# Modulation vectors of a hybrid encoder trunk, made in pairs with their columns in four blocks over the partitions

## The chip, the cores and the metric

The kernel runs on one core of a Trainium2 chip. A core has five engines with queues of their own: PE (TensorE, matrix products), DVE (VectorE), ACT (ScalarE), POOL (GpSimd) and SP (SyncE, which here issues the transfers). The metric is the device time of one execution in microseconds (us); a lower one is better.

## What is computed

Two layers over x of 1024 tokens by 1024 features. Layer 0 mixes tokens with forgetting attention (16 heads), layer 1 with gated linear attention (GLA, 4 heads); each mixer is followed by a SwiGLU with 2816 hidden features. Every sub-layer is normed and modulated by vectors that come from the conditioning vector `c`:

```python
c_act = jax.nn.silu(c)                                   # (1, 1024)
for i in range(DEPTH):                                   # 2 layers
    mod = c_act @ ada_w[i] + ada_b[i]                    # ada_w[i]: (1024, 6 * 1024)
    sh1, sc1, g1, sh2, sc2, g2 = jnp.split(mod, N_MOD, axis=-1)
    h = modulate(rms_norm(x, norm1_g[i]), sh1, sc1)      # h * (1 + sc1) + sh1
    y = mixer(h)
    x = x + g1[:, None, :] * y
    h = modulate(rms_norm(x, norm2_g[i]), sh2, sc2)
    x = x + g2[:, None, :] * swiglu(h, ffn_w_in[i], ffn_w_out[i])
return rms_norm(x, final_g)
```

The change is about `c_act @ ada_w[i]`: a vector of 1024 times a matrix of 1024 by 6144, for each layer. It is 25 MB of weights a layer, used once each, in float32.

## The kernel before

The time is mostly matrix products. Projections and the SwiGLU are done as three products of a high and a low half of each operand (`mm3`, L235 to L239), with the halves made by ACT and DVE (`split`, L159 and L160) or by ACT and POOL (`load_w`, L202 and L205). The SwiGLU (`ffn`) works with blocks whose sums and differences POOL forms from raw weights (L683 to L695); products are read out by ACT (L1410) and DVE (L1285). Weights come through `feed`, which makes them some loads ahead (`feed.depth`, 5 in the SwiGLU).

The modulation vectors are the weighted sum of the rows of `ada_w`. Vectors 0 and 1 of layer 0 are needed at once and are made by `ada0_mod`, which the change leaves alone. The others are made beside the main work by `ada_steps` (L336), one vector `j` at a time. A step `k` loads 128 rows of the matrix, one row for each partition, and multiplies each partition by its value of silu(c) (`cact[:, k:k+1]`), adding to `acc`. After the eight steps of a group, `acc` holds in each partition a partial sum, and PE adds over the partitions: `acc`'s 128 columns are the weights of a product with a column of ones (L377), which puts 128 results over the partitions, as the modulation needs them.

- Layer 0, vectors 2 to 5, in attention: a step is 128 x 1024 (512 KB, one transfer), in the ring `wr` that the weights use too; DVE multiplies and adds in four pieces of 256 columns (L367, L369). The queue `ada0` advances after each projection.
- Layer 1, vectors 0 and 1 in the SwiGLU of layer 0, vectors 2 to 5 in GLA: a group is 512 columns, a step is 128 x 512 (256 KB, one transfer, L345) into one of three buffers (SwiGLU) or two (GLA). ACT multiplies (L358 into `acc` for the first step, L360 in place for the others) and POOL adds to `acc` (L361). The load for the next step is issued ahead. The queue `ada1` is advanced by what each product is worth; a step counts `ADA_A` + `ADA_B`, 9 in the SwiGLU and 3.5 in GLA.

`acc` is one buffer in each stage. The result of L377 goes through DVE with the bias added (L379) to `modc`, and for vectors 1 and 4 `make_a` forms (1 + scale) times the norm's weight. All transfers are issued by SP, in order; an issue waits until its buffer is free. The program's order is written by hand, but the order on each engine is set at compile time by a scheduler that places work where it expects an engine to be free, so steps can run ahead of the place that the pace gives them.

At the start SP loads the first tokens of x, then rows of `c`, the biases and the norm weights (L290 to L298), which PE turns (L312, L313) so that `cact` can be made by ACT (L316).

Of the kernel before, what the change touches and what calls it, by code (L numbers as in the profile page):

```python
# [9 lines left out]
F32 = mybir.dt.float32  # L10
# [43 lines left out]
def trunk(ctx, tc, x, c, ada_w, ada_b, norm1_g, norm2_g, ffn_w_in, ffn_w_out,  # L54
          fox_w_in, fox_b_f, fox_w_out, gla_w_in, gla_w_a2, gla_b_a, gla_g_o,
          gla_w_out, final_g, out, dbg=None, stop=None):
    nc = tc.nc
    dbg = dbg or {}
    cst = ctx.enter_context(tc.tile_pool(name="cst", bufs=1))
# [49 lines left out]
    def psl(t, n=1):  # L109
        return slice(t * P, (t + n) * P)  # L110
# [40 lines left out]
    ones = cst.tile([P, 1], F32, name="ones")  # L151
    nc.vector.memset(ones, 1.0)
    mhalf = cst.tile([P, 8], F32, name="mhalf")
    nc.vector.memset(mhalf, -0.5)
    maskb = cst.tile([P, P], BF16, name="maskb")
    tri = cst.tile([P, P], I32, name="tri")

# [4 lines left out]
    wr = Ring(big, names[0:3])  # L162
# [96 lines left out]
    acc_r = Ring(big, acc_sl)  # L259
# [14 lines left out]
    def load_x(t):  # L274
        nc.sync.dma_start(xt[t], x[0, psl(t), :])
# [4 lines left out]
    def load_ada0(d):  # L280
        for kh in range(2):
# [2 lines left out]
                nc.sync.dma_start(t[:, :, j, :], adaw[0, :, 4 * kh:4 * kh + 4, j, d, :])  # L284
            araw[(d, kh)] = t

    load_x(0)
    rows2 = mrows[1][0:32]
    nc.vector.memset(rows2, 0.0)
# [40 lines left out]
    def make_a(l, i, ks=slice(0, 8)):  # L330
        j = 1 if i == 0 else 4
        g0 = 96 + i * 16 + l * 8
        nc.vector.scalar_tensor_tensor(amul[:, l, i, ks], modc[:, l, j, ks], 1.0,
                                       vec[:, g0:g0 + 8][:, ks], op0=ALU.add, op1=ALU.mult)

    def ada_steps(l, j, acc_of, raw_of, w):  # L336

        steps = deque((c0, k) for c0 in range(0, D, w) for k in range(8))
        got = deque()

        def load():
            if steps:
                c0, k = steps.popleft()
                raw = raw_of([P, w], F32, f"ada{l}{j}{c0}{k}")
                nc.sync.dma_start(raw, ada_w[l, psl(k), j * D + c0:j * D + c0 + w])  # L345
                got.append(raw)

        for c0 in range(0, D, w):
            acc = acc_of([P, w], F32, f"acc{l}{j}{c0}")
            for k in range(8):  # L350
                if w == D or c0 == k == 0:
                    load()
                raw = got.popleft()
                if w < D:
                    load()
                    yield ADA_A
                    if k == 0:
                        nc.scalar.mul(acc, raw, cact[:, 0:1])  # L358
                    else:
                        nc.scalar.mul(raw, raw, cact[:, k:k + 1])  # L360
                        nc.gpsimd.tensor_add(acc, acc, raw)  # L361
                    yield ADA_B
                    continue
                for q in range(0, w, 256):
                    cs = slice(q, q + 256)
                    if k == 0:
                        nc.vector.tensor_scalar(acc[:, cs], raw[:, cs], cact[:, 0:1], None, op0=ALU.mult)  # L367
                    else:
                        nc.vector.scalar_tensor_tensor(acc[:, cs], raw[:, cs], cact[:, k:k + 1], acc[:, cs],  # L369
                                                       op0=ALU.mult, op1=ALU.add)  # L370
                yield 1.0
            if w < D:
                yield ADA_B
            n, b = w // P, c0 // P
            mp = pj([P, n], F32, f"mp{l}{j}{c0}")
            for k in range(n):
                nc.tensor.matmul(mp[:, k:k + 1], acc[:, psl(k)], ones, start=True, stop=True)  # L377
            o = l * 48 + j * 8 + b
            nc.vector.tensor_add(modc[:, l, j, b:b + n], mp, vec[:, o:o + n])  # L379
            for i, jj in ((0, 1), (1, 4)):  # L380
                if j == jj:
                    make_a(l, i, slice(b, b + n))
        yield 1.0

    class Pace:
# [20 lines left out]

    ada0, ada1 = Pace(), Pace()

    def ada1_queue(js, acc, raws_, w):
        r = Cycle(raws_)  # L410
        for j in js:
            ada1.q.append(ada_steps(1, j, lambda *_: acc, r, w))

    mk = mrows[2]
    nc.vector.memset(mk, 0.0)
# [162 lines left out]
    sr, tr, orr, pj = ps_rings(2, 3, 1, 2)  # L578
# [229 lines left out]
    acc = first_acc(0)  # L808
# [37 lines left out]
    acc = first_acc(1)  # L846
# [1042 lines left out]
```

## Time and profile before

| | |
|---|---|
| median of 3 runs | 2449.29 us (2447.56 to 2454.5) |
| profiled execution, first to last instruction | 2446.2 us |
| transfers issued by SP for the vectors outside `ada0_mod` | 32 of 512 KB, 96 of 256 KB |
| products with ones (L377), records | 160, two for each product |
| POOL adds for the vectors (L361) | 84 |

The page gives the span of the profiled execution as its only time. Its parts are busy times of the engines, the chain of work that ended last, groups of instructions by line, and the transfers. A row of instructions reads: line, engine, operation, what it writes <- what it reads, count, then nanoseconds (least/median/most) or microseconds, and what it waited for. `issue` is time in which nothing visible was waited for.

### The profile page before, as it was taken

What the parts mean: (1) busy time and instruction counts of PE and PEld (TensorE: products, weight loads), DVE (VectorE), ACT (ScalarE), POOL (GpSimd) and SP (SyncE); (2) the same over time, 40 slices, a digit from 0 to 9 for tenths busy, and PEclk for the clock granted to TensorE, in tenths of its full rate; (3) what the DMA queues carried; (4) which work ended last, traced back from release to release, by engine and by line L of the source; (5) the groups of instructions that cost most, each with busy time, mean ns of one, the idle gap of its engine ahead of it and who ended that gap; (6) DMA issues with size and microseconds to landing.
All of it is one profiled execution on the core that took longest, in us unless ns stands there. A gap on an engine that the chain in (4) does not pass through costs nothing.

```text
span 2446.2 us, 35525 instructions
## 1 busy us (share of the span) xinstructions
PE 2385.6 (98%) x12458; PEld 2030.6 (83%) x12458; DVE 1701.0 (70%) x2849; ACT 1193.2 (49%) x2281; POOL 1151.3 (47%) x1006
## 2 busy tenths in 40 slices
PE   6999999999999999999999999999999999999998
PEld 5888888888887878888888888888888888888878
DVE  7577777676686777665788455446487677665787
ACT  4665565675454443335324765564354333345325
POOL 4233333333347786653363544443336656653262
PEclk9999999999999999999999999999999999999999
DMA  8223333223425544347665333335325434347664
GB/s 269 79 87 121 103 96 113 70 95 113 137 98 195 184 164 162 124 162 263 227 214 174 94 100 102 100 104 173 100 80 191 147 134 155 130 168 257 233 206 148
DMA packets 318203, 359.19 MB, mean 147 GB/s; under 512 B 18044, under 2 KB 246552, under 8 KB 318024
## 3 DMA queue, kind: packets, MB, share of 16 engines
q1 hardware_dynamic: 318024, 356.92, 43.7%
q8 instruction: 98, 1.61, 0.3%
q14 instruction: 81, 0.66, 0.1%
HBM read 268.19 MB, written 88.67 MB: 146 GB/s over the span
## 4 chain that ended last, share of the span: by engine, by line
PE 81%; DVE 7%; ACT 3%; DMA 3%; POOL 2%; issue 2%; SPq 1%; DVEq 0%; POOLq 0%; ACTq 0%
PE p_b L237 15%; PE p_b L239 14%; PE p_b L238 14%; PE o_b L947 2%; PE t_b L933 2%; PE qk_b L237 2%; PE qk_b L238 2%; PE qk_b L239 2%; DMA ad_s<-in_ada_w_dram 2%; PE s_b L902 1%; PE s_b L903 1%; POOL ad_s L361 1%; DVE o_s L160 1%; PE vps_b L237 1%; PE vps_b L239 1%
## 5 line engine op out<-in xcount | busy, mean ns | idle before, releaser
L160 DVE TENSOR_TENSOR o_s<-xv_s,o_s 128x512 fp32r<-128x512 f32 (+1 forms) x376 | 326.4, 872 | 86.8 <-ACT o_s L159 86.0
L159 ACT CAST o_s<-xv_s 128x512 fp32r<-128x512 f32 (+1 forms) x376 | 217.4, 587 | 308.2 <-PE p_b L239 258.5
L237 PE MATMUL p_b<-B,o_s 128*128 128x512 f32 x608 | 237.2, 393 | 7.3 <-DVE x L1285 4.9
L238 PE MATMUL p_b<-B,o_s 128*128 128x512 f32 x608 | 238.5, 392 | 0.0
L239 PE MATMUL p_b<-B,o_s 128*128 128x512 f32 x608 | 238.0, 392 | 0.0
L913 POOL TENSOR_SCALAR lp_s<-lp_s,st 128x128 f32<-128x128 f32 (+7 forms) x128 | 95.9, 754 | 294.9 <-DVE st L912 266.2
L683 POOL TENSOR_TENSOR ex_s<-xv_s,xv_s 128x512 f32<-128x512 f32 (+1 forms) x64 | 90.2, 1409 | 250.6 <-DMA xv_s<-in_ffn_w_in_dram 88.9
L237 PE MATMUL p_b<-T,o_s 128*128 128x512 f32 x480 | 187.6, 391 | 0.0
L238 PE MATMUL p_b<-T,o_s 128*128 128x512 f32 x480 | 186.9, 389 | 0.0
L239 PE MATMUL p_b<-T,o_s 128*128 128x512 f32 x480 | 182.1, 390 | 0.0
L237 PEld LDWEIGHTS p_b<-B,o_s 128*128 128x128 f32 x608 | 115.0, 189 | 32.4 <-DVE x L1285 4.2
L239 PEld LDWEIGHTS p_b<-B,o_s 128*128 128x128 f32 x608 | 115.1, 189 | 24.0
L238 PEld LDWEIGHTS p_b<-B,o_s 128*128 128x128 f32 x608 | 115.1, 189 | 23.6
L911 ACT ACTIVATE lp_s<-lp_s,st 128x128 f32<-128x128 f32 (+7 forms) x128 | 99.3, 776 | 56.3 <-DVE st L907 55.7
L1285 DVE TENSOR_TENSOR ex_s<-ex_s,p_b 128x512 f32<-128x512 f32 x140 | 94.0, 681 | 34.2 <-PE p_b L239 34.0
L159 ACT CAST pt_s<-t_b 128x512 fp32r<-128x512 f32 (+1 forms) x160 | 80.1, 547 | 71.4 <-PE t_b L933 70.2
L685 POOL TENSOR_TENSOR xv_s<-ex_s,xv_s 128x512 f32<-128x512 f32 (+1 forms) x64 | 83.5, 1305 | 63.0 <-DVE o_s L160 61.1
L160 DVE TENSOR_TENSOR pt_s<-t_b,pt_s 128x512 fp32r<-128x512 f32 (+1 forms) x160 | 96.5, 630 | 17.9 <-ACT pt_s L159 17.3
L239 PEld LDWEIGHTS p_b<-T,o_s 128*128 128x128 f32 x480 | 90.3, 188 | 19.0
L237 PEld LDWEIGHTS p_b<-T,o_s 128*128 128x128 f32 x480 | 90.2, 188 | 18.5
L238 PEld LDWEIGHTS p_b<-T,o_s 128*128 128x128 f32 x480 | 90.2, 188 | 18.4
L907 DVE CUSTOM_DVE_ANT_0 lp_s<-s_b,cum_s 128x512 f32<-128x512 f32 (+3 forms) x128 | 72.6, 569 | 40.6 <-PE t_b L933 23.0
(1939 smaller groups left out, 7543.3 us busy)
## 6 DMA issues: line engine op xcount, KB each, us to landing
xv_s<-in_ffn_w_in_dram SPq DMA_DIRECT2D x176, 256.0 KB, 3.0
hid_B<-x SPq DMA_DIRECT2D x70, 512.0 KB, 2.6
ad_s<-in_ada_w_dram SPq DMA_DIRECT2D x96, 256.0 KB, 2.9
hid_T<-x SPq DMA_DIRECT2D x36, 512.0 KB, 2.7
xv_s<-in_ffn_w_out_dram SPq DMA_DIRECT2D x96, 192.0 KB, 3.9
ada_s<-in_ada_w_dram SPq DMA_DIRECT2D x32, 512.0 KB, 3.8
xv_s<-in_ffn_w_out_dram SPq DMA_DIRECT2D x40, 256.0 KB, 2.8
T2o<-hid_T SPq DMA_DIRECT2D x18, 512.0 KB, 8.0
```

Source lines behind the costliest of these rows:

```text
L159: nc.scalar.copy(hi, src)
L160: nc.vector.tensor_sub(lo, src, hi.bitcast(F32))
L237: nc.tensor.matmul(ps, ah, bh, start=start, stop=False)
L238: nc.tensor.matmul(ps, ah, bl, start=False, stop=False)
L239: nc.tensor.matmul(ps, al, bh, start=False, stop=stop)
L683: nc.gpsimd.tensor_add(s1, a21, a22)
L685: nc.gpsimd.tensor_sub(a11, s1, a11)
L907: nc.vector.tensor_tensor_reduce(lp[:, k0:k1], ps, cm[:, k0:k1], 1.0, mcur, ALU.add, ALU.min, mnew)
L911: nc.scalar.activation(lp, lp, AF.Exp, bias=mcur, scale=-1.0, accum_out=st[:, qi, 2:3])
L913: nc.gpsimd.tensor_scalar(lp, lp, st[:, qi, 3:4], 1.0, op0=ALU.mult, op1=ALU.mult)
L933: nc.tensor.transpose(tp[:, i, :], lps[qi][:, psl(2 * b + jj)], ident)
L1285: nc.vector.tensor_add(d, d if src is None else dest(G, src), ps)
```

## The change

`ada_steps` becomes `ada_pair`: it makes two vectors, `j` and `j + 1`, together. Their 2048 columns are cut in four blocks `q` of 512. Partition 32 q + r holds block q, and it takes the 32 rows 32 r to 32 r + 31 of the matrix one after the other; a step `s` takes row 32 r + s in each. So a step is again 128 x 512 for layer 1 (and 128 x 1024, two rows, for layer 0), but a group is 32 rows long, a pair is one group, and a step's load is four transfers of 32 partitions each. The multiplier of a partition is silu(c[32 r + s]), held in a new tile `cblk` of 128 x 32, which four small loads of `c` on ACT's queue at the start and one more Silu fill. At the end PE adds over the 32 partitions of each block: the moving operand is `quart`, 128 x 4, with a one where the partition belongs to the block, so a product of 128 of `acc`'s columns gives four result columns. Four products finish a pair, where each vector took eight.

```diff
+    quart = cst.tile([P, 4], F32, name="quart")
+    nc.vector.memset(quart, 0.0)
+    for q in range(4):
+        nc.vector.memset(quart[32 * q:32 * q + 32, q:q + 1], 1.0)
...
+    craw = mrows[4][:, 0:32]
+    cblk = cst.tile([P, 32], F32, name="cblk")
+    for q in range(4):
+        nc.scalar.dma_start(craw[32 * q:32 * q + 32], c[0].rearrange("(r s) -> r s", s=32))
     load_x(0)
...
     nc.scalar.activation(cact, vps[:, P:P + 8], AF.Silu)
+    nc.scalar.activation(cblk, craw, AF.Silu)
...
-    def ada_steps(l, j, acc_of, raw_of, w):
+    def ada_pair(l, j, acc_of, raw_of, n):
+        steps = deque(range(0, 32, n))
         got = deque()
+        rows_ = ada_w[l, :, j * D:(j + 2) * D].rearrange("(r s) (q m) -> q r s m", s=32, q=4)
         def load():
             if steps:
+                s = steps.popleft()
+                raw = raw_of([P, n * HALF], F32, f"ada{l}{j}{s}")
+                for q in range(4):
+                    nc.sync.dma_start(raw[32 * q:32 * q + 32].rearrange("r (s m) -> r s m", s=n),
+                                      rows_[q, :, s:s + n])
+                got.append((s, raw))
+        acc = acc_of([P, HALF], F32, f"acc{l}{j}")
+        for i in range(0, 32, n):
+            if n > 1 or i == 0:
+                load()
+            s0, raw = got.popleft()
+            if n == 1:
+                load()
+                yield ADA_A
+                if i == 0:
+                    nc.scalar.mul(acc, raw, cblk[:, 0:1])
+                else:
+                    nc.scalar.mul(raw, raw, cblk[:, i:i + 1])
+                    nc.gpsimd.tensor_add(acc, acc, raw)
+                yield ADA_B
+                continue
+            for s in range(s0, s0 + n):
+                for c0 in range(0, HALF, 256):
...
+                        nc.vector.scalar_tensor_tensor(acc[:, cs], raw[:, rs_], cblk[:, s:s + 1], acc[:, cs],
                                                        op0=ALU.mult, op1=ALU.add)
+            yield 1.0
+        if n == 1:
+            yield ADA_B
+        mp = pj([P, 16], F32, f"mp{l}{j}")
+        for b in range(4):
+            nc.tensor.matmul(mp[:, b:16:4], acc[:, psl(b)], quart, start=True, stop=True)
+        o = l * 48 + j * 8
+        nc.vector.tensor_add(modc[:, l, j:j + 2, :].rearrange("p j k -> p (j k)"), mp, vec[:, o:o + 16])
+        if j in (0, 4):
+            make_a(l, j // 4)
...
-    for j in (2, 3, 4, 5):
-        ada0.q.append(ada_steps(0, j, acc_r, wr, D))
+    for j in (2, 4):
+        ada0.q.append(ada_pair(0, j, acc_r, wr, 2))
...
-        ada1_queue((0, 1), v[0], v[1:4], HALF)
+        ada1_queue((0,), v[0], v[1:4])
...
-    ada1_queue((2, 3, 4, 5), ada_v[0], ada_v[1:3], HALF)
+    ada1_queue((2, 4), ada_v[0], ada_v[1:3])
```

More of the change, by code (lines that the diff above doesn't have):

```diff
@@ L334, in make_a @@
                                        vec[:, g0:g0 + 8][:, ks], op0=ALU.add, op1=ALU.mult)
-    def ada_steps(l, j, acc_of, raw_of, w):
-        steps = deque((c0, k) for c0 in range(0, D, w) for k in range(8))
+    def ada_pair(l, j, acc_of, raw_of, n):
+        steps = deque(range(0, 32, n))
         got = deque()
+        rows_ = ada_w[l, :, j * D:(j + 2) * D].rearrange("(r s) (q m) -> q r s m", s=32, q=4)
         def load():
             if steps:
[L343 to L358, printed above, removed]
-                    else:
[L360 to L369, printed above, removed]
-                                                       op0=ALU.mult, op1=ALU.add)
[L371 to L382, printed above, removed]
@@ new lines, in load @@
+                s = steps.popleft()
[21 more added lines that the diff above has]
+                for c0 in range(0, HALF, 256):
+                    cs, rs_ = slice(c0, c0 + 256), slice((s - s0) * HALF + c0, (s - s0) * HALF + c0 + 256)
+                    if s == 0:
+                        nc.vector.tensor_scalar(acc[:, cs], raw[:, rs_], cblk[:, 0:1], None, op0=ALU.mult)
+                    else:
+                        nc.vector.scalar_tensor_tensor(acc[:, cs], raw[:, rs_], cblk[:, s:s + 1], acc[:, cs],
+                                                       op0=ALU.mult, op1=ALU.add)
+            yield 1.0
@@ L407, in trunk, with ada1_queue @@
     ada0, ada1 = Pace(), Pace()
-    def ada1_queue(js, acc, raws_, w):
+    def ada1_queue(js, acc, raws_):
         r = Cycle(raws_)
         for j in js:
-            ada1.q.append(ada_steps(1, j, lambda *_: acc, r, w))
+            ada1.q.append(ada_pair(1, j, lambda *_: acc, r, 1))
     mk = mrows[2]
```

## The prediction

> **What bounds the kernel now.** I read the page first: busy shares, then the chain that ended last.
>
> ```profile
> span 2446.2 us, 35525 instructions
> PE 2385.6 (98%) x12458; PEld 2030.6 (83%) x12458; DVE 1701.0 (70%) x2849; ACT 1193.2 (49%) x2281; POOL 1151.3 (47%) x1006
> ...
> PE 81%; DVE 7%; ACT 3%; DMA 3%; POOL 2%; issue 2%; SPq 1%; DVEq 0%; POOLq 0%; ACTq 0%
> ```
>
> PE is idle for 60 us of 2446 and holds 81% of the chain, so work taken from PE shortens the time unless a wait replaces it. The change touches the start and three stages, so I cut the span there (stretch, its length, busy time of each engine, then granted clock, DMA share and rate):
>
> ```profile
> 120.00:580.00 460.00, 452.65 (x2966) 397.93 (x2965) 344.95 (x908) 284.67 (x612) 163.28 (x228) 1.00 0.32 100
> 735.00:870.00 135.00, 128.71 (x562) 105.81 (x563) 94.34 (x112) 60.83 (x104) 103.49 (x70) 0.97 0.55 184
> 870.00:1060.00 190.00, 190.00 (x847) 157.57 (x846) 140.09 (x170) 76.91 (x131) 131.96 (x87) 1.00 0.45 153
> 1345.00:1660.00 315.00, 304.44 (x1863) 270.85 (x1863) 161.64 (x260) 194.40 (x398) 150.77 (x142) 0.99 0.33 101
> ```
>
> These are attention (layer 0 vectors), the SwiGLU of layer 0 (vectors 0 and 1 of layer 1; two stretches) and GLA (vectors 2 to 5). PE idles 7.4, 6.3, 0 and 10.6 us in them. PE is the bound in each; what idles lies in stretches in which vectors are being made (in the third the last of them are done by 915).
>
> **PE's products.** The products with the ones column are L377:
>
> ```profile
> L377 PE MATMUL mp_b<-ones,ad_s x96: 163/250/251, 755.2 to 1683.3; 128*128 128x1 f32 x96
> L377 PE MATMUL mp_b<-ones,acc_s x64: 164/250/251, 180.2 to 480.1; 128*128 128x1 f32 x64
> ...
> 1385.47 0.39 PE L239 MATMUL gk_b<-h1h,w_l_s 128*128 128x512 f32 x1
> 1385.70 0.95 PE L377 MATMUL mp_b<-ones,ad_s 128*128 128x1 f32 x8
> 1386.51 0.48 PE L237 MATMUL gk_b<-h1h,w_h_s 128*128 128x512 f32 x1
> ```
>
> 160 records are 80 products (two records each). The timeline shows what four of them cost: from 1385.70 to the next product's start at 1386.51 is 0.81 us. So 20 sets of four take 16.2 us now. After the change each of five pairs has four products, of four columns instead of one: 5 x 0.81 = 4.1 us. **PE gains 12.1 us**, spread over stages where it is the bound. I keep the price per product: the 128 weight columns are the same, and three more moving columns are little. Bounds of the saving: 10 us if a record with four columns cost 0.15 instead of 0.1 us, 13 us if part of the 0.81 is a hidden gap.
>
> **The transfers.** Each load becomes four, one for each 32 partitions: 128 issues on SP become 512, with the bytes unchanged.
>
> ```profile
> L345 SPq DMA_DIRECT2D ad_s<-in_ada_w_dram x96: 327/328/544, 708.6 to 1653.8; - x96
> ...
> 1.64 0.28 SPq L291 DMA_DIRECT2D mrows_s<-in_gla_g_o_dram  x1
> 1.96 0.29 SPq L292 DMA_DIRECT2D mrows_s<-in_gla_b_a_dram  x1
> 2.30 0.29 SPq L293 DMA_DIRECT2D mrows_s<-in_final_g_dram  x1
> ...
> ad_s<-in_ada_w_dram SPq DMA_DIRECT2D x96, 256.0 KB, 2.9
> ada_s<-in_ada_w_dram SPq DMA_DIRECT2D x32, 512.0 KB, 3.8
> ```
>
> An issue of 128 rows takes 0.33 us, one of 4 or 8 rows still 0.29, and those small ones start 0.33 us apart. So a quarter load costs SP nearly as much as a whole one. At 0.35 us each, 384 more issues are 134 us of SP, and the fourth quarter is issued 1.05 us after the first. A quarter lands sooner: the two landing rows differ by 0.9 us for 256 KB, which puts 128 KB at about 2.45 and 64 KB at about 2.2 us (estimates from these rows). The last quarter of a 512 KB step is then there after 1.05 + 2.45 = 3.5 us against 3.8 now; that of a 256 KB step after 3.25 against 2.9, 0.35 us later. Ends: 0 and 1.05 us (a quarter lands no sooner than a whole).
>
> [...]
>
> Behind a waiting quarter on SP stand the weight loads. SP waits in GLA for buffers far longer than the added issues (192 x 0.35 = 67 us):
>
> ```profile
> SPq L345 <- POOL ad_s L361: 118.7, 54, 9.0
> ...
> ACT ad_s L360 <- DMA ad_s<-in_ada_w_dram: 44.9, 30, 4.6
> ```
>
> That is cover for SP, but not for ACT: its queue is in order, and it already stands 44.9 us in GLA at 30 of 64 multiplications. 30 x 0.35 = 10.5 us more. All ACT waits for these loads go with at most 10.6 us of idle PE, 0.24 us for each; that caps it at 2.5 us and I take half: **+1.2 us in GLA**, ends 0 and +10 (all of the 10.5). In attention DVE waits for the loads:
>
> ```profile
>   DVE acc_s L369: 15.3, 13
> ```
>
> By the landing above this shrinks, but each step now waits for four transfers instead of one: **+0.4 us**, ends -1 and +3.
>
> **Steps of the sums.** ACT still multiplies 96 times and DVE works in 128 pieces. POOL adds 31 of 32 steps of a pair instead of 28:
>
> ```profile
> L361 POOL TENSOR_TENSOR ad_s<-ad_s,ad_s x51: 1272/1304/1845, 717.7 to 1658.2; 128x512 f32<-128x512 f32 x51
> ```
>
> Nine more adds of 1.30 us, 3 in the SwiGLU and 6 in GLA (7.8 of 164 idle us). The larger effect is when they run. The sum `acc` is one buffer, so a new group can't start before PE has read the old one. In the SwiGLU that makes bursts (POOL's adds alone, then all engines in the same stretches):
>
> ```profile
> 775.00:797.00 22.00, 10.76 (x7) 1.00 0.66 215
> 797.00:833.00 36.00, 0.00 (x0) 1.00 0.52 175
> 833.00:857.00 24.00, 11.53 (x7) 1.00 0.61 198
> ...
> 775.00:797.00 22.00, 22.00 (x99) 18.22 (x99) 14.82 (x18) 12.42 (x22) 21.66 (x15) 1.00 0.66 215
> 797.00:833.00 36.00, 36.00 (x163) 29.85 (x162) 26.61 (x32) 14.60 (x26) 23.68 (x16) 1.00 0.52 175
> 833.00:857.00 24.00, 24.00 (x110) 19.89 (x109) 17.00 (x19) 11.04 (x18) 22.99 (x15) 1.00 0.61 198
> 857.00:895.00 38.00, 35.52 (x161) 29.25 (x160) 27.69 (x33) 15.87 (x28) 26.37 (x19) 1.00 0.42 146
> ```
>
> In a burst of eight steps POOL is 96 to 98% busy, between bursts 66%; PE loses nothing inside, and 2.5 us after the third. The code paces a step to 9 us of products (`ADA_A`, `ADA_B`: 6 and 3), but the order on the engines makes one in under 3 until the group is full. A pair has one group of 32 steps instead of four of eight, so no pause: after the first eight, 24 more at 22 to 24 us for eight keep POOL full for some 70 us at a stretch, and the later half of the SwiGLU is free of it. What POOL's lateness can cost is seen here, where ACT waits for such a load, then DVE, then PE:
>
> ```profile
> 744.37 0.72 ACT L360 ACTIVATE ad_s<-ad_s,cact 128x512 f32<-128x512 f32 x1 [2.35 <-DMA ad_s<-in_ada_w_dram]
> 745.57 0.79 PE L237 MATMUL p_b<-B,o_s 128*128 128x512 f32 x1 [3.81 <-DVE x L1285]
> 745.50:750.00 4.50, 4.43 (x10) 3.47 (x11) 2.16 (x3) 2.80 (x6) 1.97 (x2) 0.50 0.72 223
> ```
>
> 3.8 us of waiting, then a granted clock of 0.50 for at least 4.5 us, in which 2.25 us of work is lost: 6 us. For the SwiGLU I take **+0.6 us**: one gap of 2.5 us goes, one of about 3 comes. Ends -2.5 and +18 (three events of 6 us).
>
> ACT also loses blocks: it waits for PE before the first multiplication of a group, up to 6.2 us:
>
> ```profile
> L358 ACTq EVENT_SEMAPHORE  x10: 17/782/6247, 711.3 to 1635.0; - x10
> ...
> 1555.86 0.72 ACT L358 ACTIVATE ad_s<-ad_s,cact 128x512 f32<-128x512 f32 x1 [4.68 <-issue]
> 1549.00:1557.00 8.00, 8.00 (x43) 6.81 (x42) 3.66 (x7) 3.02 (x6) 4.75 (x7) 1.00 0.45 131
> ```
>
> Twelve groups become three. I give this nothing: in the stretch around one of the long ones PE is busy for 8.00 of 8.00 us.
>
> **The start.** Four loads of `c` go ahead on ACT's queue:
>
> ```profile
> 0.80 0.38 SPq L275 DMA_DIRECT2D xt_s<-in_x_dram  x1
> ...
> 4.30 0.31 SPq L298 DMA_DIRECT2D mrows_s<-in_norm_g_dram  x1
> 4.30 1.06 ACT L439 ACTIVATE sq_s<-xt_s 128x1024 bf16<-128x1024 f32 x1 [2.22 <-DMA xt_s<-in_x_dram]
> 12.54 3.55 PE L462 MATMUL mp_b<-cact,adas_s 128*128 128x1 f32 x16 [4.12 <-DMA adas_s<-in_ada_w_dram]
> ```
>
> SP's ninth load starts when the first load of x has landed (ACT's square shows the moment): eight are in flight. Four small loads take four of the eight places, so the fifth load of SP, at 2.30, must wait until the first of them has landed, no earlier than about 3 us (0.8 + 2.2). PE's first real work waits for loads, so I take **+0.7 us**, ends 0 and 1.5. The Silu of 32 columns and the memsets lie in idle time there.
>
> **The sum.** -12.1 + 1.2 + 0.4 + 0.6 + 0.7 = -9.2 us on the profiled span of 2446.2, to 2437.0. The median of the runs is 2449.29, 3.1 us more, which I carry along: **2440.1 us**, 0.38% faster. About 0.3% (7.3 us) is what a measurement of this kernel can tell from no change.
>
> **The rivals.**
>
> 1. *Given back.* A quarter lands no sooner than a whole, the ACT waits of GLA grow by 30 x 1.05 = 31 us, and 0.24 of it reaches PE: +7.5 instead of +1.2; 2446.4, no change. For it: ACT is in order and the adds take turns with two buffers. Against: ACT stood 6.2 us with no gap on PE. [...]
>
> 2. *POOL overrun in the SwiGLU, slower.* Between bursts POOL's own work needs 66% of the time, inside a burst it gets 11 of 22 us, 50%. Over 70 us without a pause it falls 11 us behind, nearly the five products of 2.8 us each (12 at 0.23, the distance of the two starts at 1385) by which the weights are made ahead (`feed.depth` 5). At that point PE waits, over 3 us each time, and the clock halves. Three such events: 18 us instead of 0.6: 2449.3 - 12.1 + 2.3 + 18 = 2457.5, 0.33% slower; four, 2463. Against: POOL is given its work in an order in which the weights may come first.
>
> 3. *More than counted.* The gaps of 3.8 us with its clock loss and of 2.5 us both go, because the loads no longer stand behind pauses: 2440.1 - 0.6 - 6 - 2.5 = 2431.
>
> **How the numbers follow.** Forecast 0.46 (0.39 of it beyond 0.3%), rival 1 0.21, rival 2 0.28, rival 3 0.05. Faster 0.44, same 0.28, slower 0.28. The forecast's own range is 2434 to 2446; the asked range goes from 2432 (most of rival 3 is left out) to 2463 (rival 2 with four events; beyond it about 0.1).
>
> **What would show it.** Right: 40 records of the products instead of 160, PE's busy time near 2373; POOL's adds of the SwiGLU in one run from about 710 to 830; SP issues of about 0.3 us, 512 of them; no PE gap over 3 us in that run; ACT's waits for the loads in GLA 50 to 60 us. Wrong: a granted clock of 0.50 in several stretches between 745 and 850 (rival 2), ACT's waits in GLA over 75 us with PE's idle time there at 17 or more (rival 1), or four-column products at clearly over 0.1 us a record.

## The result, and the profile after

The changed kernel takes 2466.14 us (median of 7 runs, 2465.04 to 2468.95) against 2449.29 us for the kernel before beside it: ratio 1.0066, 95% interval 1.0052 to 1.0079. It is slower by 0.66%, where 0.38% faster was forecast; the range ended at 2463.

The page of the changed kernel, the lines that answer to those of before (busy times, then the chain of work that ended last):

```profile
span 2465.0 us, 36103 instructions
PE 2386.0 (97%) x12338; PEld 2023.1 (82%) x12338; DVE 1700.0 (69%) x2841; ACT 1192.5 (48%) x2282; POOL 1156.5 (47%) x1015
...
PE 69%; DVE 9%; DMA 7%; POOL 4%; ACT 4%; issue 4%; SPq 3%; POOLq 0%; DVEq 0%; ACTq 0%
```

120 of PE's records are gone, and yet PE is busy for 0.4 us longer and holds 69% of the chain instead of 81%. The shares of DVE and DMA in it rose by 2 and 4 points: the chain runs less through PE and more through what PE waits for. The four stretches of the prediction, in the same columns:

```profile
120.00:580.00 460.00, 449.32 (x2909) 392.62 (x2908) 337.85 (x897) 280.49 (x606) 161.75 (x225) 1.00 0.33 99
735.00:870.00 135.00, 119.33 (x505) 95.56 (x504) 95.44 (x105) 60.86 (x104) 114.59 (x76) 0.97 0.62 195
870.00:1060.00 190.00, 190.00 (x840) 157.34 (x839) 133.88 (x166) 73.24 (x126) 120.01 (x81) 1.00 0.41 140
1345.00:1660.00 315.00, 296.76 (x1785) 262.33 (x1786) 160.20 (x250) 187.70 (x382) 153.98 (x145) 0.97 0.38 106
```

PE idles 10.7 us in attention (7.4 before), 15.7 in the first part of the SwiGLU (6.3 before) and 18.2 in GLA (10.6 before). The second part of the SwiGLU, with no vectors made in it, has none.

To place the loss I counted PE's products of the kernel itself, leaving out those of the vectors, so that the n-th is nearly the same work in every kernel (12266 products in each; the order differs at about a quarter of the places), and compared when it starts in the two traces. Change against before in us, stage by stage (times of before), with the prediction's terms put where they belong: 15 sets of products fall away, 6 in attention, 3 in the SwiGLU and 6 in GLA, at 0.81 us each.

```
stage                            forecast             after
start, 0 to 113                  +0.7                 +3.6
attention, 113 to 590            -4.9 +0.4 = -4.5     +1.7
between, 590 to 686                                   -1.7
SwiGLU of layer 0, 686 to 1041   -2.4 +0.6 = -1.8     +8.0
between, 1041 to 1333                                 -0.3
GLA, 1333 to 1703                -4.9 +1.2 = -3.7     +8.1
rest                                                  -1.0
sum                              -9.3                 +18.4
```

These differences scatter: kernels in which a stage's work is unchanged differ there by up to 3.3 us, since the order on the engines is set anew for each. Each kernel also has one trace, of one execution, which need not lie at its median: of the kernels below, that of `pauses` is 5.4 us under it, that of `thin_adds` 6.3 us over it. The two of 8 us stand out.

**The products** themselves went as forecast. Their records (ns, least/median/most), and four of them in the timeline of the changed kernel:

```profile
L388 PE MATMUL mp_b<-quart,ad_s x24: 167/252/273, 827.7 to 1686.0; 128*128 128x4 f32 x24
L388 PE MATMUL mp_b<-quart,acc_s x16: 167/252/253, 286.4 to 440.1; 128*128 128x4 f32 x16
```

```profile
439.35 0.95 PE L388 MATMUL mp_b<-quart,acc_s 128*128 128x4 f32 x8
440.16 0.36 PE L957 MATMUL o_b<-pt_s,v_s 128*128 128x256 f32 x1
```

40 records in place of 160, and from 439.35 to 440.16 it is 0.81 us for four, with four columns as with one.

**The transfers:** their issue on SP (the line's records, ns), their landing (the page's transfers, median us at the end), and ACT's wait for them in GLA (us in total, times, longest):

```profile
L356 SPq DMA_DIRECT2D ad_s<-in_ada_w_dram x384: 310/419/1438, 712.2 to 1624.8; - x192
```

```profile
ad_s<-in_ada_w_dram SPq DMA_DIRECT2D x384, 64.0 KB, 2.0
```

```profile
ACT ad_s L371 <- DMA ad_s<-in_ada_w_dram: 50.4, 29, 3.8
```

An issue took 0.42 us, not 0.35, and a quarter landed in 2.0, not 2.2. The last quarter is there 3 x 0.42 + 2.0 = 3.3 us after the first issue: 0.4 us later than a whole load before (2.9), as estimated. ACT's waits in GLA are 50.4 us, inside the 50 to 60 forecast.

**The steps.** What changed is how the SwiGLU's 32 steps lie. First the kernel before, then the changed one (PE, PEld, DVE, ACT, POOL, granted clock, DMA):

```profile
745.00:775.00 30.00, 29.43 (x122) 24.17 (x123) 19.45 (x24) 11.80 (x22) 18.32 (x13) 0.90 0.41 137
775.00:800.00 25.00, 25.00 (x113) 20.70 (x113) 15.90 (x19) 13.41 (x23) 22.61 (x15) 1.00 0.61 200
```

```profile
745.00:775.00 30.00, 24.42 (x99) 19.37 (x98) 17.62 (x20) 15.40 (x26) 25.50 (x18) 0.94 0.64 184
775.00:800.00 25.00, 20.03 (x82) 15.86 (x81) 16.66 (x18) 12.31 (x22) 25.00 (x17) 0.95 0.60 187
```

Before, the first of these stretches holds a pause in the steps and the second a burst, and PE loses 0.6 us in both together. After, the adds run from 720.7 to 826.0 without a break (31 of them among 62 instructions of POOL; before, 28 among 101, from 717.7 to 912.7, with breaks of 37 to 45 us after each seven). POOL is busy for all of the 25 us, and PE loses 10.5 of 55 us. One of its gaps, in the timeline of the changed kernel:

```profile
754.88 1.28 POOL L372 TENSOR_TENSOR ad_s<-ad_s 128x512 f32<-128x512 f32 x1 [0.86 <-DMA ad_s<-in_ada_w_dram]
...
756.12 1.72 POOL L694 TENSOR_TENSOR xv_s<-xv_s 128x512 f32<-128x512 f32 x1
...
757.24 0.72 ACT L371 ACTIVATE ad_s<-ad_s,cblk 128x512 f32<-128x512 f32 x1 [1.36 <-DMA ad_s<-in_ada_w_dram]
...
757.87 0.60 ACT L163 CAST o_s<-xv_s 128x512 fp32r<-128x512 f32 x1
...
758.52 0.50 PE L241 MATMUL p_b<-T,o_s 128*128 128x512 f32 x1 [3.03 <-ACT o_s L163]
```

POOL makes a weight (L694) behind an add for the vectors that had itself waited 0.86 us for its load, ACT casts it (L163) behind a multiplication that waited 1.36 us for the next one, and PE waits 3.03 us for the cast. There are five gaps of over 1.8 us between 745 and 820, of 2.56, 3.03, 2.17, 2.80 and 1.87 us; before, there were two in the whole of 735 to 870, of 3.81 and 2.48. The other four end with DVE, which reads a product out (L1295); PE's waits from 740 to 830:

```profile
PE p_b L241 <- DVE ex_s L1295: 4.7, 3, 2.2
PE p_b L241 <- DVE x L1295: 3.2, 2, 2.6
PE p_b L241 <- ACT o_s L163: 3.0, 1, 3.0
PE p_b L241 <- DVE sg_s L1295: 2.8, 1, 2.8
```

The readout stands in DVE's queue behind the low halves of the weights (L164), and these mostly wait for ACT's cast. At 781.67, for example, ACT stood 1.70 us at a multiplication whose load wasn't there, DVE then 1.82 us for the cast behind it, and PE 2.17 us for DVE. Before 796.77 no such wait is seen: there DVE works without a break from 791.29 on, and POOL is full.

In GLA, the same columns of the changed kernel, and then POOL's adds alone in two of the stretches:

```profile
1400.00:1440.00 40.00, 36.66 (x186) 29.98 (x185) 23.92 (x33) 28.21 (x66) 23.62 (x20) 1.00 0.47 128
1440.00:1480.00 40.00, 35.84 (x268) 33.27 (x267) 23.39 (x41) 27.34 (x59) 21.29 (x21) 1.00 0.36 98
1480.00:1530.00 50.00, 50.00 (x266) 42.84 (x265) 24.17 (x44) 21.75 (x49) 12.12 (x16) 1.00 0.21 60
...
1580.00:1635.00 55.00, 48.16 (x256) 40.22 (x256) 27.07 (x43) 32.90 (x63) 31.39 (x29) 0.94 0.42 111
```

```profile
1480.00:1530.00 50.00, 1.30 (x1) 1.00 0.21 60
...
1580.00:1635.00 55.00, 21.46 (x17) 0.94 0.42 111
```

PE idles 3.3, 4.2 and 6.8 us in three stretches inside the two runs of adds (1362.6 to 1475.3 and 1527.9 to 1629.7), and not at all between them. POOL isn't full here. At the two largest gaps (2.30 us up to 1423.28, 3.10 up to 1627.64) ACT's queue is what is late; the second in the timeline:

```profile
1625.35 0.72 ACT L371 ACTIVATE ad_s<-ad_s,cblk 128x512 f32<-128x512 f32 x1 [2.66 <-DMA ad_s<-in_ada_w_dram]
...
1627.00 0.58 ACT L1771 ACTIVATE gs_s<-gr_b 128x512 f32<-128x512 f32 x1
```

ACT stands 2.66 us at a multiplication, and PE then waits 3.10 us for ACT's `gs_s`, which stood behind it.

### The profile page after: what moved, and what is told of

It is laid out like the page before. It is cut to its first block, busy times and chain, and to the rows that moved or that the text cites. A ratio compares the mean times of both kernels' runs of the same rounds, so it can differ in the third digit from the quotient of the medians.

```text
span 2465.0 us, 36103 instructions
## 1 busy us (share of the span) xinstructions
PE 2386.0 (97%) x12338; PEld 2023.1 (82%) x12338; DVE 1700.0 (69%) x2841; ACT 1192.5 (48%) x2282; POOL 1156.5 (47%) x1015
## 4 chain that ended last, share of the span: by engine, by line
PE 69%; DVE 9%; DMA 7%; POOL 4%; ACT 4%; issue 4%; SPq 3%; POOLq 0%; DVEq 0%; ACTq 0%
PE p_b L241 13%; PE p_b L243 13%; PE p_b L242 13%; DMA ad_s<-in_ada_w_dram 3%; SPq L356 2%; PE o_b L957 2%; PE t_b L943 2%; POOL ad_s L372 2%; PE qk_b L241 1%; PE qk_b L242 1%; PE qk_b L243 1%; DMA ada_s<-in_ada_w_dram 1%; DVE o_s L164 1%; PE s_b L912 1%; PE s_b L913 1%
## 5 line engine op out<-in xcount | busy, mean ns | idle before, releaser
L164 DVE TENSOR_TENSOR o_s<-xv_s,o_s 128x512 fp32r<-128x512 f32 (+1 forms) x376 | 327.9, 875 | 87.4 <-ACT o_s L163 87.0
L163 ACT CAST o_s<-xv_s 128x512 fp32r<-128x512 f32 (+1 forms) x376 | 217.7, 586 | 319.6 <-PE p_b L243 257.9
L1295 DVE TENSOR_TENSOR ex_s<-ex_s,p_b 128x512 f32<-128x512 f32 x140 | 93.8, 681 | 33.2 <-PE p_b L243 33.0
L163 ACT CAST pt_s<-t_b 128x512 fp32r<-128x512 f32 (+1 forms) x160 | 79.8, 548 | 63.3 <-PE t_b L943 62.4
L371 ACT ACTIVATE ad_s<-ad_s,cblk 128x512 f32<-128x512 f32 x93 | 67.0, 721 | 83.8 <-DMA ad_s<-in_ada_w_dram 80.3
L164 DVE TENSOR_TENSOR pt_s<-t_b,pt_s 128x512 fp32r<-128x512 f32 (+1 forms) x160 | 96.3, 631 | 10.8 <-ACT pt_s L163 10.3
```

What stands on the lines that cost most here:

```text
L163: nc.scalar.copy(hi, src)
L164: nc.vector.tensor_sub(lo, src, hi.bitcast(F32))
L371: nc.scalar.mul(raw, raw, cblk[:, i:i + 1])
L1295: nc.vector.tensor_add(d, d if src is None else dest(G, src), ps)
```

## The experiments

Two theories came from the traces. **A:** the quarter loads cost (four issues and four landings a step). **B:** the pair's one sum makes 32 steps run without the pause that the kernel before had every eight steps, and in that run the kernel's own work on POOL, ACT and DVE falls behind. The start's loads of `c` are a third, smaller suspect. A ratio below is always to the kernel before, run beside the experiment.

### The loads alone

`one_load` keeps the change but loads a step whole, with the columns' block in the partition's lowest two bits (`quart` and `cblk` to match); `before_quarters` splits the loads of the kernel before in four.

```diff
-        rows_ = ada_w[l, :, j * D:(j + 2) * D].rearrange("(r s) (q m) -> q r s m", s=32, q=4)
+        rows_ = ada_w[l, :, j * D:(j + 2) * D].rearrange("(r s) (q m) -> r q s m", s=32, q=4)
...
-                for q in range(4):
-                    nc.sync.dma_start(raw[32 * q:32 * q + 32]...
+                for i in range(n):
+                    nc.sync.dma_start(raw[:, i * HALF:(i + 1) * HALF], rows_[:, :, s + i])
```

> The changed kernel with one transfer of 128 partitions a step in place of four of 32 (partition 4 r + q holds row block r and column block q; in attention two transfers a step, one for each row), everything else kept. Theory A (the quarter transfers cost: SP is busy with four issues, the last quarter lands later, ACT and DVE stand in their queues): nearly all of the 17 us come back, with the products' saving on top: 2440 to 2450 us, ACT's waits for the loads in GLA 40 us or less. Theory B (the missing pauses cost: 32 steps in one run keep POOL full in the SwiGLU): the gaps of PE between 740 and 830 stay, 2457 to 2466 us.

```diff
-                nc.sync.dma_start(raw, ada_w[l, psl(k), j * D + c0:j * D + c0 + w])
+                for q in range(4):
+                    r0 = k * P + 32 * q
+                    nc.sync.dma_start(raw[32 * q:32 * q + 32], ada_w[l, r0:r0 + 32, j * D + c0:j * D + c0 + w])
```

> The kernel before with each load of the vectors cut into four transfers of 32 partitions and nothing else changed: groups of eight steps, pauses and 80 products stay. Theory A: slower by what the change lost and the 12 us of products besides, 2460 to 2475 us. Theory B: 2449 to 2453 us, since the pauses are there.

`one_load`: 2462.65 us, 1.0052 of before (1.0035 to 1.0069). `before_quarters`: 2444.88, 0.9974 (0.9961 to 0.9986). Theory A falls as the main cause: whole loads take back 3.5 of the 16.9 us, and 384 more issues in the kernel before cost nothing; that kernel has the lowest median of all here. By the count, `one_load` is at +3.9 in the SwiGLU, where 8.0 were lost, and at +6.7 in GLA. So about half of the SwiGLU's loss went with the quarters, or with the order that the scheduler made of the other loads; this run doesn't tell the two apart. The stretches 735 to 870 and 1345 to 1660 of `one_load` lie between those of the changed kernel and those before, in GLA almost at the former:

```profile
735.00:870.00 135.00, 123.48 (x523) 98.92 (x523) 101.12 (x111) 62.77 (x106) 117.22 (x78) 0.97 0.61 202
...
1345.00:1660.00 315.00, 297.30 (x1787) 261.75 (x1787) 159.60 (x249) 189.28 (x388) 151.77 (x146) 0.98 0.35 103
```

### The start alone

`start_only` is the kernel before with `quart`, the four loads of `c` and the Silu; `one_c` is the changed kernel with one load of `c` on SP's queue behind the loads of the first vectors.

```diff
+    for q in range(4):
+        nc.scalar.dma_start(craw[32 * q:32 * q + 32], c[0].rearrange("(r s) -> r s", s=32))
...
+    nc.scalar.activation(cblk, craw, AF.Silu)
```

> The kernel before with only the start of the change: the four loads of c ahead of the first load of x, the Silu of 32 columns and the memsets; their results are not used. If the first 112 us, in which the changed kernel fell 3.6 us behind, are the cost of these loads: 2452 to 2455 us, with PE's first product at about 7 us instead of 4.8. If that loss came from the order that the compile-time scheduler chose: 2447 to 2451 us.

```diff
-    for q in range(4):
-        nc.scalar.dma_start(craw[32 * q:32 * q + 32], c[0].rearrange("(r s) -> r s", s=32))
+    nc.sync.dma_start(craw, c[0].rearrange("(r s) -> r s", s=32).unsqueeze(0).to_broadcast([4, 32, 32]))
```

> The changed kernel with the four loads of c ahead of x replaced by one on SP behind the first x and vector loads. Theory of the start (four of the eight places are taken): PE's first product at about 5 us again and 3 to 5 us come back: 2461 to 2463 us. If the start is a matter of the compile-time order: 2465 us or more.

`start_only`: 2456.58, 1.0023 (1.0011 to 1.0036), about 5.6 us, with PE's first product at 7.23. `one_c`: 2471.33, 1.0089 (1.0076 to 1.0102); it gave nothing back. The timeline of the changed kernel shows the mechanism that was forecast (SP's loads, then PE's first product; after it that product in the kernel before and in `one_c`):

```profile
2.13 0.28 SPq L299 DMA_DIRECT2D mrows_s<-in_gla_g_o_dram  x1
4.05 0.25 SPq L300 DMA_DIRECT2D mrows_s<-in_gla_b_a_dram  x1
...
7.13 0.28 PE L320 MATMUL vps_b<-ident,mrows_s 32*128 32x32 f32 x1 [7.13 <-DMA mrows_s<-in_final_g_dram]
```

```profile
4.83 0.28 PE L312 MATMUL vps_b<-ident,mrows_s 32*128 32x32 f32 x1 [4.83 <-DMA mrows_s<-in_final_g_dram]
```

```profile
6.42 0.28 PE L319 MATMUL vps_b<-ident,mrows_s 32*128 32x32 f32 x1 [6.42 <-DMA mrows_s<-in_final_g_dram]
```

Four loads on ACT's queue and four on SP's have been issued by 2.63, and SP's fifth starts only at 4.05; PE's first product is at 7.13 instead of 4.83. Without the four loads, in `one_c` and in `pauses_late` further down, it is still at 6.42: there, as in the changed kernel, two of x's loads of 512 KB come first on SP, where the kernel before had one. So of the 2.3 us the four loads account for 0.7, and the new order of the other loads for 1.6.

### The steps: shorter adds, and the old pauses

`thin_adds` has POOL's adds of layer 1 run over 32 columns and leaves the other 480 out of the sums; `pair_by_eights` puts the sum out after every eight steps, as before, with 36 products more in layer 1.

```diff
-                    nc.gpsimd.tensor_add(acc, acc, raw)
+                    nc.gpsimd.tensor_add(acc[:, 0:32], acc[:, 0:32], raw[:, 0:32])
```

> The changed kernel with POOL's adds for layer 1's vectors over 32 of 512 columns (the rest of each sum is left out, so those vectors are incomplete); transfers, multiplications and products stay. Theory B: POOL is no longer full in the SwiGLU, PE's gaps between 745 and 830 go: 2455 to 2460 us. Theory A: the gaps stay, since ACT still waits for the quarters: 2463 to 2467 us.

```diff
-                if i == 0:
-                    nc.scalar.mul(acc, raw, cblk[:, 0:1])
+                if i % 8 == 0:
+                    nc.scalar.mul(acc, raw, cblk[:, i:i + 1])
...
+                if i % 8 == 7 and i < 31:
+                    yield ADA_B
+                    drain(i == 7)
```

> The changed kernel with layer 1's sums drained after every eight steps (four products, DVE adds the result to modc), so that a step must again wait for PE after each eight; the quarter transfers, the pair layout and the loads of c stay, layer 0 stays a group of 32. Products for layer 1: 48 as in the kernel before. Theory B (the unbroken run of POOL's adds is the loss, in the SwiGLU and in GLA): 2450 to 2456 us, the rest over the kernel before being the start, although PE gets 7 us of products back. Rival C (the quarters or the pair layout load the SwiGLU and GLA in another way): 2463 us or more.

`thin_adds`: 2448.12, 0.9985 (0.9973 to 0.9997). `pair_by_eights`: 2450.24, 1.0007 (0.9996 to 1.0017). By the same count as above, the SwiGLU is at -3.3 and +0.7, GLA at -0.3 and -2.4, with loads, `c` and pairs as in the changed kernel. Against what the products alone would give (-2.4 and -4.9 in `thin_adds`, nothing in `pair_by_eights`), the loss of both stages is gone but for 4.6 us in GLA of `thin_adds`. Theory B holds, though `pair_by_eights` left open whether the pause did it or the sum begun afresh.

### The order on POOL

`paced` holds each add behind the POOL instruction that is written before it, so that the scheduler can't draw the adds together; `paced_one_c` adds the load of `one_c`.

```diff
-                    nc.gpsimd.tensor_add(acc, acc, raw)
+                    with tc.issue_after(last_on("G")):
+                        nc.gpsimd.tensor_add(acc, acc, raw)
```

> The changed kernel with POOL's adds held in the order of the program on POOL: an add is queued behind the POOL work that the program gave before it, which spreads the SwiGLU's 31 adds over some 146 of POOL's instructions in place of 60; GLA's adds keep about their places. Nothing is removed. Theory B: the SwiGLU gives back its 8 us, GLA keeps its 8: 2456 to 2460 us. If only the number of adds counts, and not when they run: 2464 us or more.

> Both of the last two: paced adds and one load of c. If the two losses are separate they add up: 2451 to 2456 us. If they aren't: no better than the better of the two.

`paced`: 2459.3, 1.005 (1.0035 to 1.0065). `paced_one_c`: 2462.42, 1.0052 (1.004 to 1.0064). The time of `paced` is the expected one by luck: expected was that the SwiGLU gives its 8 us back and GLA keeps its own, and it came the other way. The adds of the SwiGLU now lie among 149 POOL instructions (732 to 1042 us), and GLA gave back 7.7 us (+0.4). The SwiGLU keeps +6.7, in another form; PE's waits between 700 and 1041:

```profile
PE p_b L241 <- ACT o_s L163: 11.3, 6, 3.0
```

Held in order, POOL stands at an add whose load isn't there and delays the weights behind it: a gap of 1.5 to 3.0 us about every 41 us. Spreading the adds isn't enough; they also must not be waited for.

### Pauses alone

`pauses` is the changed kernel in which the multiplication of steps 8, 16 and 24 waits for the PE instruction written just before it. Nothing else differs: 12 products for layer 1, one sum, quarter loads.

```diff
+                    pe = last_on("P") if i % 8 == 0 else None
                     nc.scalar.mul(raw, raw, cblk[:, i:i + 1])
+                    if pe is not None:
+                        ...   # the multiplication waits for pe
                     nc.gpsimd.tensor_add(acc, acc, raw)
```

> After, with three pauses put into each pair of layer 1: the multiplication of steps 8, 16 and 24 waits, in the order of the engines, for the PE instruction written just before it. Nothing else is changed: the same loads, the same 12 products for these pairs, no extra sum buffer. Theory B (the loss is that 32 multiplications and adds run without a pause and fill POOL, and PE's products wait behind it): the SwiGLU and GLA give back about 8 us each, the time is 2446 to 2453, with 128 to 129 us of PE in 735 to 870 and 303 or more in 1345 to 1660. This differs from the kernel with a product every eight steps, which took pauses and products together. Rival (the pauses are not it; the extra products or the sums begun afresh were): 2463 or more, with PE as in after. Rival C (a pause helps only if it comes as late as a sum buffer is read): between, 2455 to 2460.

2445.54, 0.9987 (0.9972 to 1.0002): 20.6 us below the changed kernel (19 by the two ratios). By the count, the SwiGLU is at -3.9 and GLA at -5.1 against before, about the products' share of -2.4 and -4.9. The two stretches of `pauses`:

```profile
735.00:870.00 135.00, 129.99 (x567) 105.99 (x568) 98.49 (x116) 57.99 (x101) 97.04 (x65) 1.00 0.55 177
...
1345.00:1660.00 315.00, 305.37 (x1848) 269.16 (x1847) 163.86 (x261) 197.63 (x404) 158.99 (x149) 1.00 0.37 106
```

PE is back at 130.0 and 305.4 us, above the kernel before (128.7 and 304.4), and the granted clock is 1.00. The adds of the SwiGLU now come in four bursts (717.8 to 744.1, 809.9 to 833.7, 888.2 to 911.4 and 965.8 to 989.2). This settles it for the kernel: three waits a pair undo the loss, with the loads, the products and the one sum as they were. What a pause does inside it, letting POOL, ACT and DVE catch up or holding the steps near the place that the pace gives them, isn't told apart. ACT's waits for the loads in GLA are 53.8 us here, more than in the changed kernel (50.4): their total says nothing; what counts is whether they come bunched.

> The kernel with one load a step in place of four, with the same three pauses for each pair. Theory B: as with pauses alone, the SwiGLU and GLA give back what they lose in the kernel with one load (3.9 and 6.8 us): 2446 to 2453. If the number of loads mattered once the pauses are there, it is 3 us or more below the kernel with pauses; if it does not, within 2 us of it.

With one load a step and the same pauses: 2446.01, 0.9986 (0.9973 to 0.9999). The pauses give 16.6 us here too, and once they are there the number of loads makes no difference.

> The kernel with pauses, and the four loads of c and the Silu over 32 columns moved from the start to just before the first vectors of layer 0 are queued. If the loss at the start (first product 2.3 us later, 0.23% for the start's part done alone) comes from the four loads standing among the first eight, the first product is back at 4.8 us and the time is 2 to 4 us below the kernel with pauses: 2443 to 2449. If the start's loss was an accident of the order of the loads, it is the same as the kernel with pauses within 2 us.

With the loads of `c` moved behind the start: 2448.89, 0.9995 (0.9983 to 1.0008). The expected 2 to 4 us didn't come; the first product is at 6.42, as in `one_c`, the start to 113 us is 1.1 us shorter than in `pauses`, and later stages lost that again.

### The steps on DVE

```diff
-                    nc.scalar.mul(raw, raw, cblk[:, i:i + 1])
-                    nc.gpsimd.tensor_add(acc, acc, raw)
+                    nc.vector.scalar_tensor_tensor(acc, raw, cblk[:, i:i + 1], acc, op0=ALU.mult, op1=ALU.add)
```

> After, with each step of layer 1 as one fused multiply-add on DVE in place of ACT's multiplication and POOL's add; loads and products as in after. Theory B (POOL's unbroken adds are the loss): PE in 735 to 870 goes from 119.3 back to 127 or more and GLA from 296.8 to 303, the time is 2448 to 2456, unless DVE (69% busy, some 0.6 to 0.7 us for each of 96 steps more) becomes what PE waits for there. Rival (any unbroken run of 32 steps costs this, on whatever engine): 2463 or more, with PE's gaps now ended by DVE.

2460.85, 1.0052 (1.0034 to 1.007): between the two. The SwiGLU is at +0.9, so there the steps on ACT and POOL were most of the loss; GLA stays at +5.9, with its 64 steps taken off ACT and POOL and DVE busy for 191.9 of 315 us (160.2 in the changed kernel). PE's longest wait there is now one of 2.6 us for DVE. That fits a run that costs on whichever engine carries it, but it isn't shown: DVE is also simply busier.

### Attention

`attn_whole`, `pauses_whole` and `pauses_whole_late` load attention's steps by two transfers of 128 partitions in the change's own order (block by block), in the changed kernel, in `pauses` and in `pauses_late`.

```diff
+                if n == 2:
+                    for i in range(n):
+                        nc.sync.dma_start(raw[:, i * HALF:(i + 1) * HALF], rows_[:, :, s + i])
```

> After, with the steps of attention (two rows for each partition) loaded by two transfers of 128 partitions in place of four of 32; layer 1 as in after. Theory L (in attention the quarter loads come late enough that DVE waits 10 us more for them, and its queue, in order, makes PE wait 2.7 us for a reduction at about 303): DVE's waits for these loads in attention go from 22.8 to about 14 us, the wait of 2.68 shrinks under 2, and attention gives back 3 to 5 us: 2461 to 2463. Rival (the wait at 303 comes from the order on DVE and would be there with any loads): attention as in after within 1.5 us, 2465 to 2467.

> The kernel with pauses, with the steps of attention loaded whole. Theory L: 3 to 4 us below the kernel with pauses (2445.5): 2441 to 2443, ratio to before about 0.997. Rival: the same as the kernel with pauses within 2 us.

> As the kernel before this in the list, and the four loads of c and their Silu moved to just before the vectors of layer 0. If the start's four loads cost what the start's part alone did (5.6 us at the end, 2.4 at the first product), 2436 to 2441. Rival (as found when only this was added to the pauses: nothing gained): 2441 to 2446.

2535.12, 2516.78 and 2508.99 us, 1.0338 (1.0324 to 1.0352), 1.0262 (1.0248 to 1.0277) and 1.023 (1.0216 to 1.0244): 60 to 71 us slower than the same kernels with quarter loads, all expectations missed. DVE's waits for the loads in attention, in the changed kernel, then in `attn_whole`:

```profile
DVE acc_s L381 <- DMA ada_s<-in_ada_w_dram: 22.8, 16, 3.2
```

```profile
DVE acc_s L385 <- DMA ada_s<-in_ada_w_dram: 83.7, 43, 4.3
```

A stretch of `attn_whole` in which such a transfer is alone, and one of `one_load`, where the block is innermost in the partition and a weight load shares the engines (the last two columns are the busy share of the 16 DMA engines and GB/s):

```profile
220.00:221.00 1.00, 1.00 (x9) 0.73 (x8) 0.55 (x2) 0.00 (x0) 0.00 (x0) 1.00 0.27 102
```

```profile
231.00:234.00 3.00, 3.00 (x20) 2.65 (x19) 1.07 (x4) 0.00 (x0) 0.58 (x1) 1.00 0.81 265
```

The same 256 pieces of 2 KB, two transfers, start over 6.4 us (216.2 to 222.6), at 0.27 of the engines, about four of sixteen, when the outermost index of the source has four values, and over 2.0 us (231.5 to 233.6), at 0.81, when it has 32. So this layout can't be loaded whole at speed, and the three runs say nothing of the question they were made for. Other traces say something: the wait of PE for DVE at about 303 us is 2.7 us long in the changed kernel, is missing in the kernel before and in `before_quarters` (quarter loads without pairs), and is 1.4 us in `one_load` (pairs with whole loads). DVE's waits for the loads are 22.8, 12.5, 13.8 and 14.3 us in these four. This points to the pairs as what brings the wait, and to the quarter loads as what lengthens it. With whole loads attention is at -3.9, but the start at +7.4; by 590 us 1.8 us are left of that gain.

## Why the prediction was wrong

- *Products, -12.1:* right in price and count (0.81 us for four). In `pauses` this saving reaches the time in the SwiGLU and GLA; in the changed kernel it is eaten. The sign "PE's busy time near 2373" missed (2386.0), though; in `pauses` it is 2377.6.
- *SwiGLU, +0.6, ends -2.5 and +18:* the step that failed. It saw that a pair has no pause and that POOL stays full, and priced that with one gap of 3 us. Net of the 2.4 us of products it cost 10.4: five gaps of 1.9 to 3.0 us where there were two, and a halved clock behind two of the five. Rival 2 named this mechanism and the gaps and clock that would show it; its price of 18 us was too high for one stage, four of the five gaps end with DVE's readout and not with a weight, and it stopped at the SwiGLU.
- *GLA, +1.2, ends 0 and +10:* failed too. It counted ACT's waits, and these came as counted (50.4 us). But the same lost pauses make two runs there, and that cost 13.0 us net of the products. The sign "PE's idle time at 17 or more" came true (18.2), the one beside it (ACT's waits above 75) did not, and with whole loads GLA stays at +6.7, so rival 1's cause is out. The 0.24 us of PE for each us of ACT's waits was no price: `pauses` has more of these waits and 8.6 us less idle PE (9.6 against 18.2).
- *ACT's waits at a group's first multiplication, "nothing":* right that they cost PE nothing before, but they were the pauses. What a wait holds back has to be priced when it goes.
- *Transfers:* right for layer 1 (0.4 us later for the last quarter; quarters in the kernel before cost nothing). For two halves of the partitions the page "DMA: Bandwidth & Descriptors" of the Trainium skill, section "Rules for kernel authors", has one transfer of 128 partitions instead. In this kernel quarters cost nothing beside it (`before_quarters` at 0.9974; `pauses` and `one_load_pauses` at 0.9987 and 0.9986); `attn_whole` bears on the order of its source and not on this rule.
- *Attention, +0.4, ends -1 and +3:* outside its ends, with 6.6 net of the 4.9. DVE's waits grew instead of shrinking, and one wait of 2.68 us of PE for a reduction on DVE at 303, with the clock halved behind it, took most of the 4.9. The cause is argued from the traces and not shown.
- *Start, +0.7, ends 0 and +1.5:* the four loads cost the 0.7 forecast at the first product (7.13 against 6.42 without them). The other 1.6 of its 2.3 us come from the order of x's loads, which the forecast took as unchanged; by 113 us it is 3.6.

Of the 27.7 us between forecast and count, 9.8 are in the SwiGLU, 11.8 in GLA and 9.1 before 590; the rest gave 3.0 back.

## What to carry to other kernels

A buffer that makes a side task wait also sets its pace: before merging groups, look at what the waits between them kept apart, and where longer groups save something, put the pause back by itself (three waits a pair were worth some 20 us here). Price background work on shared engines by how densely it lies, not by its busy time or the total of its waits, which hardly differ between the good and the bad kernel. And split a transfer so that its outermost index has many values, or give each block its own transfer.

## What the runs showed of the hardware

A gap's length didn't decide alone whether the clock halved. In the changed kernel it halved behind gaps of 2.68, 2.80 and 3.03 us and not behind one of 2.56; in `paced` it halved behind one of 1.82 us and not behind one of 3.04. The traces show why: the granted clock changes only on a grid of 3.41 us, in each of the seventeen (in the changed kernel the half clock sets in at 33.01, 67.14, 80.80, 306.08, 760.05 and 797.60 us, whole multiples of 3.413 apart), and what counts is how much of a gap falls into one field of the grid. In pairs, the field with most of the gap and the one after it (PE's busy time comes after the length, the granted clock is the third value from the end); first the gap of 2.56 and that of 3.03 in the changed kernel, then those of 3.04 and 1.82 in `paced`:

```profile
746.40:749.81 3.41, 1.65 (x7) 1.40 (x8) 1.63 (x2) 1.20 (x3) 2.23 (x2) 1.00 0.57 161
749.81:753.22 3.41, 3.41 (x16) 2.81 (x16) 0.95 (x1) 1.71 (x3) 2.02 (x2) 1.00 0.75 204
756.64:760.05 3.41, 1.53 (x7) 1.27 (x8) 2.21 (x4) 2.28 (x4) 3.41 (x3) 1.00 0.56 147
760.05:763.46 3.41, 3.41 (x10) 2.64 (x9) 2.46 (x3) 0.71 (x2) 3.33 (x3) 0.50 0.64 182
```

```profile
872.84:876.26 3.42, 1.75 (x8) 1.43 (x9) 1.77 (x3) 2.79 (x5) 0.00 (x0) 1.00 0.00 0
876.26:879.67 3.41, 3.41 (x17) 2.81 (x15) 1.58 (x4) 0.91 (x2) 1.67 (x1) 1.00 0.26 77
992.31:995.72 3.41, 1.59 (x8) 1.00 (x7) 1.37 (x3) 1.65 (x3) 1.27 (x1) 1.00 0.24 76
995.72:999.14 3.42, 3.42 (x10) 2.65 (x9) 2.70 (x5) 1.14 (x3) 1.24 (x1) 0.50 0.27 79
```

PE idled 1.76, 1.88, 1.67 and 1.82 us in the first of each pair. Counted over all traces from 20 us on, each of the 83 fields at full clock with 1.94 us or more of idle PE was followed by one at half clock, and 43 of the 88 with 1.5 to 1.93 us. So were 55 of 11689 with less idle PE; why is open.

The Trainium skill, "TensorE: Matmul & The Clock Gate", section "What's actually happening", has the clock follow a free-running window of about 3.4 us, which agrees with the grid. It also has the clock halve after an idle window; in these rows a window of which PE idled 1.82 us was enough. The forecast's 6 us for an event were too many in the SwiGLU: 3.03 us of gap and 1.7 lost in 3.4 us of half clock make 4.7. The gap of 3.10 us in GLA did cost 6.2, since the half clock lasted for two fields (1627.0 to 1633.9).

A transfer of 64 KB landed in 2.0 us, where one of 256 KB had taken 2.9. DVE's `o_s` operations in 735 to 870 got longer the busier POOL was: 1041 ns before with POOL busy for 77% of the stretch, 1139 after with 85%, and 914 in `thin_adds` with 62%:

```profile
L160 DVE TENSOR_TENSOR o_s<-xv_s,o_s 128x512 fp32r<-128x512 f32 x41 | 42.5, 1041 | 20.5 <-ACT o_s L159 20.1 <-DMA xv_s<-in_ffn_w_in_dram 0.4
```

```profile
L164 DVE TENSOR_TENSOR o_s<-xv_s,o_s 128x512 fp32r<-128x512 f32 x37 | 42.1, 1139 | 24.5 <-ACT o_s L163 24.5
```

```profile
L164 DVE TENSOR_TENSOR o_s<-xv_s,o_s 128x512 fp32r<-128x512 f32 x40 | 36.5, 914 | 21.8 <-ACT o_s L163 21.7
```

The Trainium skill, "GPSIMD Engine Reference", section "1. Specifications", says that GpSimd shares its SBUF interfaces with VectorE; these rows agree with it.
